# Three rotating PSUM tiles for the projections, three for the indexer logits, and the second half's gates moved ahead of branch B's pools

## The chip, the cores and the metric

The kernel runs on one core of a Trainium2 chip. The metric is the device time of one execution in microseconds, the median of several runs. The engines are named as in the profile: PE (TensorE), DVE (VectorE), ACT (ScalarE), POOL (GpSimd) and SP (SyncE, which issues the DMAs). Each engine takes its own instructions in the order in which the program lists them.

## What is computed

One layer over 2,048 tokens of width 1,024. A layer norm gives h; one projection of h (7,592 columns) feeds three branches and their gates; branch A attends to 256 keys per token that an indexer selects.

```
h = layer_norm(x)
a_q, a_k, a_v, a_gate, i_q, i_k, i_w, b_q, b_k, b_v, b_gate, c_q, c_gate, m_gate = split(h @ w_in)
# A: 8 heads over the top 256 keys of an indexer score
score = einsum('bqh,bqhs->bqs', i_w, relu(einsum('bqhd,bsd->bqhs', i_q, i_k)))   # chunk-causal
idx   = top_k(score, 256)
o_a   = softmax(a_q @ a_k[idx]) @ a_v[idx]
# B: differential attention, 4 heads;  C: attention into 256 memory tokens, 4 heads
merged = sum of sigmoid(m_gate[r]) * ((o_r * silu(gate_r)) @ w_proj[r])
out    = layer_norm(2**0.25 * h + merged @ w_out)
```

## The kernel before

**Stages.** The 16 blocks of 128 tokens are taken in two halves. For each half the kernel transposes h into H4 (`prologue`), projects the queries and the indexer (`dense_ai`), projects keys, values and queries of branch B (`dense_b`) and later the gates (`gates`). Every product of 32-bit accuracy is three matmuls (`mm3`, lines 77 to 79). A projection's result stands in a PSUM tile called dps; ACT and DVE read it out, and then the tile is free for the next projection. One tile of the gates takes 24 matmuls of 512 columns.

**The top-k search.** `topk_group` is called three times: for blocks 2 to 7, 8 to 11 and 12 to 15. A call has three parts. First the indexer logits: a PE matmul pair into a PSUM tile called ips (line 514), a Relu by ACT (line 519), and an accumulation into sall by DVE (line 523). Then a search of 32 passes for the threshold, one bit a pass: DVE counts for two of the blocks (line 550), ACT for the other two (line 563), and DVE forms the bit (line 567). At last a tie-break by block: POOL marks equal scores (line 595), DVE scans, selects and forms the mask (lines 598 to 601), and SP stores it (line 602). All this needs DVE, ACT and POOL; PE is needed for the logits alone. So the search stands beside projections, which keep PE busy meanwhile.

**What sets the order.** A scheduler orders each engine's instructions at build time from the program, its priorities and its own estimate of when a tile's buffer comes free; on the chip the order is fixed. Branch B's PE order is written out by hand (`tc.manual_schedule`). SP's queue holds all DMAs in one order.

**Around the change.** The projections' PSUM pool is `dqs` with 2 tiles (dps). `dq2` has 2 tiles for transposes (psT). `tq` has 4 tiles for the logits (ips), and `q1`, which stands there earlier, 4 for the first transposes. That is all 8 banks. After the third search comes `dense_b(1)`, then the pools are released, branch B's pools are made (`bp` in SBUF, `lgp` and `bs` in PSUM), then the second half's gates run, then four jobs of the first half's gates, and then branch B, whose first matmul is lg of line 655. Its keys kg, values vg and queries bq are loaded by SP into `bp`, which lies where the search's tiles lay.

Of the kernel before, what the change touches and what calls it, by code (L numbers as in the profile page):

```python
# [9 lines left out]
F32 = mybir.dt.float32  # L10
# [48 lines left out]
def tile_layer(ctx, tc, x, mem, ln_in_g, ln_in_b, w_in, w_mem_kv, diff_lambda, diff_norm_g,  # L59
# [101 lines left out]
    p1 = pool("p1", 3)  # L161
    dp = pool("dp", 2)
    dqs = pool("dqs", 2, PSUM)
    dq2 = pool("dq2", 2, PSUM)
    q1 = pool("q1", 2, PSUM, "right")
    xp = pool("xp", 8, side="right")
# [80 lines left out]
    def dense(kind, half, cols, idx, w=None):  # L247
        n = sum(c for _, c in cols)
        if w is None:
            w = load_win(cols, A if early[0] else G)  # L250
        for p in range(4 * half, 4 * half + 4):
            ps = dqs.tile([128, 2, 256], F32, name="dps")
            for i in range(2):
                h = hT_of(2 * p + i)
                for k in range(KT):
                    mm3(ps[:, i, :n], h[:, 0, k], h[:, 1, k], w[:, 0, k, :n], w[:, 1, k, :n], k == 0, k == KT - 1)
            with tc.high_priority():
                emit(kind, idx, p, ps, n)

    def gate_steps(kind, half, c0, idx, w=None, qs=(0, 1)):  # L260
        if w is None:
            w = load_win([(c0, 256)])
        for q in (2 * half + q for q in qs):
            for g in range(2):
                c = slice(g * 128, (g + 1) * 128)
                ps = dqs.tile([128, 512], F32, name="dps")
                for k in range(KT):
                    mm3(ps, w[:, 0, k, c], w[:, 1, k, c], H4[:, q % 2, 0, k], H4[:, q % 2, 1, k], k == 0, k == KT - 1)
                    if k == KT - 1:
                        with tc.high_priority():  # L270
                            emit_gate(kind, idx, g, q, ps)
                    yield 0.69

    def dense_ai01(half):
        W = []
        for i in range(2):
            if half == 0 and i:
                w = xw.tile([128, 2, 4, W_AI], F32R, name="w1", bufs=1)
            else:
                w = dw.tile([128, 2, KT, 256], F32R, name="w")  # L280
                w = w.rearrange("p a k c -> p (a k c)")[:, :8 * W_AI].rearrange("p (a k c) -> p a k c", a=2, k=4)
            W.append(w)
            if half:
                SP.dma_start(w.bitcast(F32), w_d["ai", i])
                continue
            for c0, cols in ((0, [(C_AK, 128), (C_IQ, 128)]), (256, [(C_IQ + 128, W_AI - 256)])):
                n = sum(c for _, c in cols)
                for k in (0, 2):
                    raw = dw.tile([128, 2, 256], F32, name="wr", bufs=2)
                    o0 = 0  # L290
                    for a0, an in cols:
                        SP.dma_start(raw[:, :, o0:o0 + an], w_view(w_in, i * 512 + k * 128, 2, a0, an))
                        o0 += an
                    split(w[:, 0, k:k + 2, c0:c0 + n], w[:, 1, k:k + 2, c0:c0 + n], raw[:, :, :n], A, G)
            w_d["ai", i] = dram(f"w_dai{i}", [128, 2, 4, W_AI])
            SP.dma_start(w_d["ai", i], w.bitcast(F32))
        for p in range(4 * half, 4 * half + 4):
            ps = [dqs.tile([128, 512], F32, name="dps") for _ in range(2)]
            for a in range(2):
                for i in range(2):  # L300
                    h = hT_of(2 * p + i)
                    for k in range(4):
                        kk = 4 * a + k
                        mm3(ps[i][:, :W_AI], h[:, 0, kk], h[:, 1, kk], W[a][:, 0, k], W[a][:, 1, k], kk == 0, kk == KT - 1)
            with tc.high_priority():
                o = [dw.tile([128, 2, 256], F32, name="do", bufs=3) for _ in range(2)]
                with tc.high_priority():
                    for i in range(2):
                        A.copy(o[0][:, i], ps[i][:, :256])
                        A.copy(o[1][:, i, :W_AI - 256], ps[i][:, 256:W_AI])  # L310
                emit("ai0", None, p, None, 256, o[0])
                emit("ai1", None, p, None, W_AI - 256, o[1])
# [97 lines left out]
    def run(steps):  # L410
        for _ in steps:
            pass
# [45 lines left out]
            W0 = load_win([(C_AQ, 256)], A, G, xw)  # L458
    SP.dma_start(rp, rope.rearrange("(b p) c -> p b c", p=128))
    for b in range(8):  # L460
        prologue(b, [(q1, "psT", 4)])
    dense_ai(0)
    rope0 = last_rope[0]
    xw.release()
    xp.release()
    q1.release()
    tk = pool("tk", 1, side="right")
    tq = pool("tq", 4, PSUM, "right")
    KI = {}

    def load_ki(half):
# [138 lines left out]
    for b in range(8, NB):  # L610
        load_x(b, p1)
        with tc.high_priority():
            prologue(b, [(tq, "ips", 4)])
    dense_ai(1)
    load_ki(1)
    topk_group([8, 9, 10, 11])
# [20 lines left out]

    dp.release()
    p1.release()
    dq2.release()  # L640

    bp = pool("bp", 2, side="right")
    lgp = pool("lgp", 2, PSUM, "right")
    turn = [0]
    bs = pool("bs", 1, PSUM, "right")
# [151 lines left out]
            G.tensor_scalar(o, o, rs, None, op0=ALU.mult)  # L797
            SP.dma_start(ob_d[b][:, hd * 128:(hd + 1) * 128], o)

    run(gates(1, JOBS[:-2]))  # L800
    run(gates_by_tokens(1, JOBS[-2:]))
    for p in range(4):
        with tc.high_priority():
            reload(p)
# [389 lines left out]
```

## Time and profile before

| | us |
|---|---|
| median of 3 runs | 2905.12 (2904.59 to 2905.88) |
| the profiled execution, its own time | 2899.8 |
| its span in the trace | 2898.0 |
| PE busy | 2767.6 (95%) |
| DVE busy | 2053.2 (71%) |
| ACT busy | 1401.0 (48%) |
| POOL busy | 861.0 (30%) |

The span is the time from the first to the last instruction that the trace shows; the execution's own time has 1.8 us around it. Matmuls overlap in their pipeline and the trace models their ends, so a busy PE can still hold short gaps. Times within the trace are counted from the span's start.

### The profile page before, as it was taken

Reading aid. Unit: us, or ns where it says so; the run is one execution under the profiler, and the core shown is the slowest. Engines: PE = TensorE matmul, PEld = TensorE weight load, DVE = VectorE, ACT = ScalarE, POOL = GpSimd, SP = SyncE. Lnnn points to the kernel's source line nnn. Section 1 sums busy time; section 2 is a strip of 40 time slices with the busy share of each in tenths; the row PEclk is TensorE's granted clock in tenths of the full one; section 3 lists DMA queues with packets and bytes.
Section 4 is the critical chain, followed back from the end, with each engine's and each line's share of the span. In section 5 each row is a group of like instructions: output and inputs, shape, how many; then the busy total and the mean of one; then the engine's idle time right before and its main releaser. Section 6 shows DMA issues by size and latency. Waiting matters only on the chain.

```text
span 2898.0 us, 49105 instructions
## 1 busy us (share of the span) xinstructions
PE 2767.6 (95%) x17488; PEld 2486.4 (86%) x17488; DVE 2053.2 (71%) x4885; ACT 1401.0 (48%) x2716; POOL 861.0 (30%) x1270
## 2 busy tenths in 40 slices
PE   7899999999999998999999999999999999988998
PEld 6799989987788877788878887888999999987887
DVE  7179977899657887577777773547777777775654
ACT  3256755774245881344444442446565655552110
POOL 7454333235433312023232323301222222211322
PEclk9999999999999999999999999999999999998999
DMA  9766654474645575534333425254333334358642
GB/s 359 237 211 233 206 185 165 157 251 149 219 151 174 203 275 182 175 107 130 128 118 113 146 80 171 91 178 133 103 112 104 104 114 124 115 175 262 210 153 73
DMA packets 332021, 476.35 MB, mean 164 GB/s; under 512 B 28929, under 2 KB 252545, under 8 KB 323585
## 3 DMA queue, kind: packets, MB, share of 16 engines
q1 hardware_dynamic: 331776, 473.23, 49.9%
q8 instruction: 138, 2.26, 0.3%
q14 instruction: 107, 0.87, 0.1%
HBM read 271.25 MB, written 201.88 MB: 163 GB/s over the span
## 4 chain that ended last, share of the span: by engine, by line
PE 68%; DMA 7%; DVE 7%; issue 3%; POOL 2%; ACT 2%; SPq 0%; DVEq 0%; POOLq 0%; ACTq 0%
PE dps L77 9%; PE dps L78 9%; PE dps L79 9%; PE ops L760 4%; PE aops L906 4%; PE apt L901 3%; PE lg L655 3%; PE lg L656 3%; PE pt L768 2%; PE yps L77 2%; PE yps L78 2%; PE yps L79 2%; PE fz L77 2%; PE fz L79 2%; PE fz L78 2%
## 5 line engine op out<-in xcount | busy, mean ns | idle before, releaser
L77 PE MATMUL dps<-H,w 128*128 128x512 f32 x1280 | 517.9, 405 | 20.8 <-DVE do L329 6.8
L78 PE MATMUL dps<-H,w 128*128 128x512 f32 x1280 | 504.9, 394 | 0.0
L79 PE MATMUL dps<-H,w 128*128 128x512 f32 x1280 | 503.7, 394 | 0.0
L77 PE MATMUL dps<-w,H 128*128 128x256 f32 (+1 forms) x1152 | 342.5, 298 | 16.3 <-ACT w L71 8.8
L79 PE MATMUL dps<-w,H 128*128 128x256 f32 (+1 forms) x1152 | 340.2, 296 | 2.0 <-DVE H L74 1.9
L78 PE MATMUL dps<-w,H 128*128 128x256 f32 (+1 forms) x1152 | 340.9, 296 | 0.8 <-POOL w L74 0.8
L563 ACT ACTIVATE ja<-sall,thr 128x1280 bf16<-128x1280 f32 (+4 forms) x224 | 301.8, 1347 | 74.5 <-DVE thr L559 69.0
L550 DVE TENSOR_SCALAR_CACHE_REDUCE jd<-sall,thr 128x1408 bf16<-128x1408 f32 (+6 forms) x231 | 330.8, 1432 | 6.3
L77 PEld LDWEIGHTS dps<-H,w 128*128 128x128 f32 x1280 | 243.3, 190 | 66.0 <-DVE do L329 7.4
L79 PEld LDWEIGHTS dps<-H,w 128*128 128x128 f32 x1280 | 242.7, 190 | 51.4
L78 PEld LDWEIGHTS dps<-H,w 128*128 128x128 f32 x1280 | 243.6, 190 | 38.2
L658 DVE CUSTOM_DVE_ANT_0 AP<-lg,bias 128x512 f32<-128x512 f32 (+3 forms) x304 | 181.7, 619 | 107.6 <-PE lg L656 50.2
L523 DVE SCALAR_TENSOR_TENSOR sall<-ir,iw,sall 128x512 f32<-128x512 f32 (+3 forms) x266 | 191.9, 768 | 70.0 <-ACT ir L519 67.5
L77 PEld LDWEIGHTS dps<-w,H 128*128 128x128 f32 x1152 | 224.0, 195 | 19.0 <-ACT w L71 9.4
L71 ACT CAST apr<-apt 128x512 fp32r<-128x512 f32 (+1 forms) x288 | 157.3, 562 | 153.2 <-PE apt L901 122.6
L79 PEld LDWEIGHTS dps<-w,H 128*128 128x128 f32 x1152 | 223.6, 194 | 3.3 <-DVE H L74 2.5
L78 PEld LDWEIGHTS dps<-w,H 128*128 128x128 f32 x1152 | 223.7, 194 | 2.6 <-POOL w L74 1.8
L74 DVE TENSOR_TENSOR apr<-apt,apr 128x512 fp32r<-128x512 f32 (+1 forms) x288 | 185.5, 656 | 56.7 <-ACT apr L71 54.9
L906 PE MATMUL aops<-apr,VA 128*128 128x256 f32 x1088 | 202.9, 294 | 11.8 <-DVE ao L916 6.2
L893 ACT ACTIVATE AP<-AP,anm 128x1024 f32<-128x1024 f32 (+7 forms) x192 | 172.2, 899 | 75.9 <-DVE anm L890 75.2
L519 ACT ACTIVATE ir<-ips 128x512 f32<-128x512 f32 (+3 forms) x304 | 149.9, 550 | 105.9 <-PE ips L514 91.5
L734 ACT ACTIVATE P<-P,nm 128x2048 f32<-128x2048 f32 (+15 forms) x128 | 154.4, 1206 | 85.8 <-DVE nm L733 85.7
(250 smaller groups left out, 6760.5 us busy)
## 6 DMA issues: line engine op xcount, KB each, us to landing
w_d<-w SPq DMA_DIRECT2D x28, 2048.0 KB, 7.3
w<-w_d SPq DMA_DIRECT2D x28, 2048.0 KB, 9.0
wr<-in_w_in_dram SPq DMA_DIRECT2D x108, 256.0 KB, 3.2
tm_d<-do SPq DMA_DIRECT2D x96, 256.0 KB, 2.6
bq<-qb_d SPq DMA_DIRECT2D x128, 128.0 KB, 3.3
aq<-qa_d SPq DMA_DIRECT2D x128, 128.0 KB, 3.0
yt<-tm_d SPq DMA_DIRECT2D x64, 256.0 KB, 3.4
sg_d<-do SPq DMA_DIRECT2D x48, 256.0 KB, 2.7
```

What stands on the lines that cost most here:

```text
L71: A.copy(H, src)
L74: el.tensor_tensor(L, src, H.bitcast(F32), op=ALU.subtract)
L77: PE.matmul(ps, lH, rH, start=start, stop=False)
L78: PE.matmul(ps, lH, rL, start=False, stop=False)
L79: PE.matmul(ps, lL, rH, start=False, stop=stop)
L523: V.scalar_tensor_tensor(s[:, c0:c0 + cn], r[:, :cn], iw[:, h:h + 1], s[:, c0:c0 + cn], op0=ALU.mult, op1=ALU.add)
L550: V.tensor_scalar(jd[:, :L], sc[b], t.bitcast(F32)[:, i:i + 1], None, op0=op, op1=ALU.add, accum_out=dst[:, i:i + 1])
L563: A.activation(ja[:, :L], sc[b], AF.Sign, bias=thr.bitcast(F32)[:, i:i + 1], scale=-1.0, accum_out=cnt[:, i:i + 1])
L658: V.tensor_tensor_reduce(P[:, c0:c0 + cn], ps[:, :cn], bias[:, c0:c0 + cn], scale=-0.125, scalar=-LOW, op0=ALU.add, op1=ALU.min, accum_out ...
L734: A.activation(p[:, :L], p[:, :L], AF.Exp, bias=nm[:, c:c + 1], scale=-1.0, accum_out=sm[:, c:c + 1])
L893: A.activation(p[:, c0:c1], p[:, c0:c1], AF.Exp, bias=nm[:, e:e + 1], scale=-1.0, accum_out=sm[:, hd, i:i + 1])
L906: PE.matmul(o_ps.rearrange("p a d -> p (a d)"), VA[:, k0 + i], pr[:, a, i].rearrange("p e q -> p (e q)"), start=(k0 + i == 0 and a == 0), ...
```

## The change

A helper `bank` gives the projections their PSUM tile: every third one is a new tile called dpx, one buffer in the pool `dq2`, and the others are dps as before. It does so until `spare[1]` is set to False, after the second half's gates. To make room, the logits have three ips tiles in place of four, and the early transposes three in place of four. The second half's gates are written ahead of the release of `dq2`, so ahead of branch B's PSUM pools; `bp` is now made ahead of them.

```diff
--- before.py
+++ after.py
@@ -161,6 +161,14 @@
     p1 = pool("p1", 3)
     dp = pool("dp", 2)
     dqs = pool("dqs", 2, PSUM)
+    spare = [0, True]
+
+    def bank(shape):
+        spare[0] += 1
+        if spare[1] and spare[0] % 3 == 0:
+            return dq2.tile(shape, F32, name="dpx", bufs=1)
+        return dqs.tile(shape, F32, name="dps")
+
     dq2 = pool("dq2", 2, PSUM)
     q1 = pool("q1", 2, PSUM, "right")
     xp = pool("xp", 8, side="right")
@@ -249,7 +257,7 @@
         if w is None:
             w = load_win(cols, A if early[0] else G)
         for p in range(4 * half, 4 * half + 4):
-            ps = dqs.tile([128, 2, 256], F32, name="dps")
+            ps = bank([128, 2, 256])
             for i in range(2):
                 h = hT_of(2 * p + i)
                 for k in range(KT):
@@ -263,7 +271,7 @@
         for q in (2 * half + q for q in qs):
             for g in range(2):
                 c = slice(g * 128, (g + 1) * 128)
-                ps = dqs.tile([128, 512], F32, name="dps")
+                ps = bank([128, 512])
                 for k in range(KT):
                     mm3(ps, w[:, 0, k, c], w[:, 1, k, c], H4[:, q % 2, 0, k], H4[:, q % 2, 1, k], k == 0, k == KT - 1)
                     if k == KT - 1:
@@ -295,7 +303,7 @@
             w_d["ai", i] = dram(f"w_dai{i}", [128, 2, 4, W_AI])
             SP.dma_start(w_d["ai", i], w.bitcast(F32))
         for p in range(4 * half, 4 * half + 4):
-            ps = [dqs.tile([128, 512], F32, name="dps") for _ in range(2)]
+            ps = [bank([128, 512]) for _ in range(2)]
             for a in range(2):
                 for i in range(2):
                     h = hT_of(2 * p + i)
@@ -458,14 +466,14 @@
             W0 = load_win([(C_AQ, 256)], A, G, xw)
     SP.dma_start(rp, rope.rearrange("(b p) c -> p b c", p=128))
     for b in range(8):
-        prologue(b, [(q1, "psT", 4)])
+        prologue(b, [(q1, "psT", 3)])
     dense_ai(0)
     rope0 = last_rope[0]
     xw.release()
     xp.release()
     q1.release()
     tk = pool("tk", 1, side="right")
-    tq = pool("tq", 4, PSUM, "right")
+    tq = pool("tq", 3, PSUM, "right")
     KI = {}
 
     def load_ki(half):
@@ -610,7 +618,7 @@
     for b in range(8, NB):
         load_x(b, p1)
         with tc.high_priority():
-            prologue(b, [(tq, "ips", 4)])
+            prologue(b, [(tq, "ips", 3)])
     dense_ai(1)
     load_ki(1)
     topk_group([8, 9, 10, 11])
@@ -637,9 +645,12 @@
 
     dp.release()
     p1.release()
+
+    bp = pool("bp", 2, side="right")
+    run(gates(1, JOBS[:-2]))
+    run(gates_by_tokens(1, JOBS[-2:]))
+    spare[1] = False
     dq2.release()
-
-    bp = pool("bp", 2, side="right")
     lgp = pool("lgp", 2, PSUM, "right")
     turn = [0]
     bs = pool("bs", 1, PSUM, "right")
@@ -797,8 +808,6 @@
             G.tensor_scalar(o, o, rs, None, op0=ALU.mult)
             SP.dma_start(ob_d[b][:, hd * 128:(hd + 1) * 128], o)
 
-    run(gates(1, JOBS[:-2]))
-    run(gates_by_tokens(1, JOBS[-2:]))
     for p in range(4):
         with tc.high_priority():
             reload(p)
```

How the order on the engines moves is shown at two places. The names carry the tiles' numbers, which are the same in both kernels; line numbers behind the new helper are 8 higher after the change, and 11 higher in branch B.

The first place is PE, the last indexer logits of the third group (ips_6803) among the second half's gates. Before:

```order
L514 MATMUL ips_6792<-KI3_1551,qi_6625 128x256
L77 MATMUL dps_10398<-H4_257,w_10379 128x512
L514 MATMUL ips_6797<-KI4_5198,qi_6625 128x256
L514 MATMUL ips_6797<-KI5_5200,qi_6625 128x256
L514 MATMUL ips_6803<-KI6_5202,qi_6625 128x256
L514 MATMUL ips_6803<-KI7_5204,qi_6625 128x256
L78 MATMUL dps_10398<-H4_257,w_10379 128x512
L79 MATMUL dps_10398<-H4_257,w_10379 128x512
```

And after the change:

```order
L79 MATMUL dpx_10943<-H4_257,w_10896 128x512
L77 MATMUL dpx_10943<-H4_257,w_10896 128x512
L522 MATMUL ips_6797<-KI4_5198,qi_6625 128x256
L522 MATMUL ips_6797<-KI5_5200,qi_6625 128x256
L522 MATMUL ips_6803<-KI6_5202,qi_6625 128x256
L522 MATMUL ips_6803<-KI7_5204,qi_6625 128x256
L78 MATMUL dpx_10943<-H4_257,w_10896 128x512
L79 MATMUL dpx_10943<-H4_257,w_10896 128x512
```

The last logits stand in the projection tile numbered 10398 before, and in tile 10943 now, 17 projection tiles further on. In the whole order 4,720 projection matmuls stand ahead of the last logit before, and 5,122 now; ahead of branch B's first lg stand 5,805 in both.

The second place is DVE, the tie-break of the third group. Lines 322 and 329 are evictions of projection tiles, line 550 a count. Before, for block 14:

```order
L550 TENSOR_SCALAR jd_6821,cnt_6818<-sall_6068,tf_7068 128x1920
L322 TENSOR_TENSOR do_11549<-dps_11521,do_11546 128x512
L597 TENSOR_SCALAR need_7073<-cnt_6818 128x1
L329 SCALAR_TENSOR_TENSOR do_11579<-do_11579,dps_11554 128x512
L598 SCALAR_TENSOR_TENSOR pf_6822<-ones_1541,ja_6820 128x1920
L329 SCALAR_TENSOR_TENSOR do_11608<-do_11608,dps_11583 128x512
L599 SCALAR_TENSOR_TENSOR ja_6820<-pf_6822,need_7073,ja_6820 128x1920
L600 TENSOR_TENSOR ja_6820<-ja_6820,jd_6821 128x1920
L601 TENSOR_SCALAR pf_6822<-ja_6820 128x1920
L550 TENSOR_SCALAR jd_6821,cnt_6818<-sall_6068,tf_7068 128x2048
L329 SCALAR_TENSOR_TENSOR do_11637<-do_11637,dps_11612 128x512
```

After the change, first the place where the last eviction ahead of branch B stands (line 337, tile dps_11816), among the search's passes:

```order
L558 TENSOR_SCALAR jd_6821,cnt_6818<-sall_6068,thr_6817 128x1920
L575 TENSOR_TENSOR bit_6819<-cnt_6818,lim_6811 128x4
L337 SCALAR_TENSOR_TENSOR do_11841<-do_11841,dps_11816 128x512
L576 SCALAR_TENSOR_TENSOR pre_6809<-bit_6819,pre_6809 128x4
L567 SCALAR_TENSOR_TENSOR thr_6817<-pre_6809,flip_6816 128x4
L558 TENSOR_SCALAR jd_6821,cnt_6818<-sall_6068,thr_6817 128x1664
L558 TENSOR_SCALAR jd_6821,cnt_6818<-sall_6068,thr_6817 128x1920
L575 TENSOR_TENSOR bit_6819<-cnt_6818,lim_6811 128x4
```

And after the change the end of the tie-break, for block 15, and the first instruction for branch B (lg_11876):

```order
L558 TENSOR_SCALAR jd_6821,cnt_6818<-sall_6068,tf_7068 128x2048
L605 TENSOR_SCALAR need_7073<-cnt_6818 128x1
L606 SCALAR_TENSOR_TENSOR pf_6822<-ones_1541,ja_6820 128x2048
L607 SCALAR_TENSOR_TENSOR ja_6820<-pf_6822,need_7073,ja_6820 128x2048
L608 TENSOR_TENSOR ja_6820<-ja_6820,jd_6821 128x2048
L609 TENSOR_SCALAR pf_6822<-ja_6820 128x2048
L674 TENSOR_SCALAR P_11875,mx_11872<-lg_11876 128x384
L676 ISA P_11875,mx_11872<-lg_11876,diag_249 128x128
L676 ISA mx_11872 128x1
L337 SCALAR_TENSOR_TENSOR do_11884<-do_11884,dps_11845 128x512
```

Before, 15 evictions stand from the search's last bit to branch B's first instruction, between the instructions of the tie-break and behind it. Now all of them stand ahead of the search's last four passes, and these passes and the whole tie-break follow behind the eviction of dps_11816 with nothing between. On SP the four mask stores stand likewise in a row, straight ahead of branch B's first key load, where before eleven stores of gates stood among them. PE has 21 matmuls of its next tile, dps_11845, between dps_11816 and the first lg, in both kernels.

## Rows read from the trace of the kernel before

**Rows 1.** Page, part 1: busy us, share of the span, instructions

```profile
PE 2767.6 (95%) x17488; PEld 2486.4 (86%) x17488; DVE 2053.2 (71%) x4885; ACT 1401.0 (48%) x2716; POOL 861.0 (30%) x1270
```

**Rows 2.** Waits of TensorE, 145 to 1181 us: total, times, longest

```profile
PE dps L77 <- DVE do L329: 6.8, 6, 2.0
...
PE dps L77 <- DVE do L322: 4.5, 2, 2.5
...
PE dps L77 <- DVE need L597: 4.3, 1, 4.3
...
PE dps L77 <- DVE de L74: 3.1, 2, 2.1
...
PE dps L77 <- DVE thr L559: 3.0, 1, 3.0
```

**Rows 3.** Line 514, logits of groups two and three: ns; first, last start

```profile
L514 PE MATMUL ips<-KI,qi x183: 219/280/388, 404.9 to 542.6; 128*128 128x256 f32 x166, 128*128 128x128 f32 x17
...
L514 PE MATMUL ips<-KI,qi x233: 221/279/283, 755.3 to 916.7; 128*128 128x256 f32 x105, 128*128 128x128 f32 x12
```

**Rows 4.** Line 602, bias stores of groups two and three

```profile
L602 SPq DMA_DIRECT2D bias_d<-pf x4: 319/380/586, 712.6 to 754.8; - x4
...
L602 SPq DMA_DIRECT2D bias_d<-pf x4: 319/320/933, 1110.9 to 1157.1; - x4
```

**Rows 5.** Chain of waits, 1080 to 1200 us: start, us, what

```profile
1098.57 4.49 POOL ja L595
...
1124.07 8.91 DMA bias_d<-pf
...
1141.91 5.45 POOL ja L595
...
1168.23 9.38 DMA kg<-kb_d
...
1177.62 4.92 DMA bq<-qb_d
...
1182.68 0.47 PE lg L656
```

**Rows 6.** Line 567, one bit of the third search each

```profile
L567 DVE TENSOR_TENSOR bit<-cnt,lim x32: 149/164/165, 924.6 to 1090.6; 128x4 int32<-128x4 f32 x32
```

**Rows 7.** Timeline of ScalarE near branch B: start, us, instruction

```profile
1170.71 0.60 ACT L327 ACTIVATE do<-dps 128x512 f32<-128x512 f32 x1 [4.84 <-PE dps L79]
...
1176.15 0.60 ACT L327 ACTIVATE do<-dps 128x512 f32<-128x512 f32 x1 [4.84 <-PE dps L79]
```

**Rows 8.** Timeline of VectorE, four counts and an eviction

```profile
1064.41 1.95 DVE L550 TENSOR_SCALAR_CACHE_REDUCE jd<-sall,thr 128x1664 bf16<-128x1664 f32 x1
...
1069.45 1.95 DVE L550 TENSOR_SCALAR_CACHE_REDUCE jd<-sall,thr 128x1664 bf16<-128x1664 f32 x1
...
1073.58 0.69 DVE L322 TENSOR_TENSOR do<-dps,do 128x512 fp32r<-128x512 f32 x1
...
1075.69 1.95 DVE L550 TENSOR_SCALAR_CACHE_REDUCE jd<-sall,thr 128x1664 bf16<-128x1664 f32 x1
```

**Rows 9.** Five lines of the last tie-break: ns of one, first, last start

```profile
L595 POOL TENSOR_SCALAR ja<-sall,tf x4: 4484/4956/5436, 1098.6 to 1141.9; 128x1664 bf16<-128x1664 f32 x1, 128x1792 bf16<-128x1792 f32 x1, 128x1920 bf16<-128x1920 f32 x1, 128x2048 bf16<-128x2048 f32 x1
...
L598 DVE TENSOR_TENSOR_SCAN pf<-ones,ja x4: 3625/4026/4425, 1103.1 to 1147.4; 128x1664 f16<-128x1664 bf16 x1, 128x1792 f16<-128x1792 bf16 x1, 128x1920 f16<-128x1920 bf16 x1, 128x2048 f16<-128x2048 bf16 x1
...
L599 DVE SCALAR_TENSOR_TENSOR ja<-pf,need,ja x4: 1952/2144/2347, 1106.7 to 1152.3; 128x1664 bf16<-128x1664 f16 x1, 128x1792 bf16<-128x1792 f16 x1, 128x1920 bf16<-128x1920 f16 x1, 128x2048 bf16<-128x2048 f16 x1
...
L600 DVE TENSOR_TENSOR ja<-ja,jd x4: 1015/1125/1225, 1109.2 to 1154.7; 128x1664 bf16<-128x1664 bf16 x1, 128x1792 bf16<-128x1792 bf16 x1, 128x1920 bf16<-128x1920 bf16 x1, 128x2048 bf16<-128x2048 bf16 x1
...
L601 DVE TENSOR_SCALAR pf<-ja x4: 594/643/689, 1110.3 to 1156.4; 128x1664 bf16<-128x1664 bf16 x1, 128x1792 bf16<-128x1792 bf16 x1, 128x1920 bf16<-128x1920 bf16 x1, 128x2048 bf16<-128x2048 bf16 x1
```

**Rows 10.** Windows, all engines: busy us, PEclk, DMA share, GB/s

```profile
1082.00:1086.00 4.00, 4.00 (x12) 3.12 (x11) 3.40 (x8) 2.71 (x5) 0.00 (x0) 0.57 0.94 388
...
1157.00:1182.00 25.00, 24.34 (x106) 19.59 (x104) 2.87 (x5) 2.40 (x4) 0.00 (x0) 0.99 0.95 263
```


## The prediction

> **What bounds the kernel now.** I read the page first. PE is busy 95% of the span [rows 1], so at first sight only PE's gaps could be won. The waits of TensorE between 145 us (where the first indexer logits come) and 1181 us (where branch B begins) show which gaps the rotation aims at: PE waited for DVE before a projection tile 6.8 + 4.5 + 4.3 + 3.1 + 3.0 = 21.7 us in all [rows 2]. That is everything a third tile could give back, apart from clock. After such a wait the granted clock can fall to half: around 1082 us, behind such a wait, the mean over 4 us is 0.57 [rows 10], between the two levels of 1.2 and 2.4 GHz, which costs 4 x 0.43 = 1.7 us. There are four such places in this part (near 727, 1082, 1109 and 1154 us), 7 us together.
>
> Then I read the search as a chain of its own, because it runs beside PE. It is a chain without slack. The last mask of group two is stored at 754.8 us [rows 4] and the first logit of group three starts at 755.3 [rows 3]. The last mask of group three is stored at 1157.1 [rows 4], SP then loads keys, values and queries, and the second lg matmul runs at 1182.7, having waited for bq [rows 5]. The chain of waits of that stretch goes through POOL, the mask store and the loads, not through PE alone [rows 5]. So at 1181 us two chains end together: PE's projections, and the search with its loads. A change is to be judged by both. The search can be late by next to nothing before PE waits for it, since PE's list goes on with lg and cannot pass it.
>
> **The change part by part.** *The third projection tile* can give back at most the 21.7 us of [rows 2]. Some of it counts only if it comes ahead of the search's last logits, because later the search decides. Of the five rows, 4.3 and 3.1 us and a part of the 6.8 and 4.5 lie earlier. I take 6 us, between 0 and 13.
>
> *The fourth logits tile* is what the change takes away, and the order shows what that does. The scheduler places a pair of logits where it thinks a tile is free; with three tiles it places them further apart. Counted in the order of PE, the last logit of group one comes behind 1,055 projection matmuls before and 1,225 now, that of group two behind 3,070 and 3,389, that of group three behind 4,720 and 5,122: each group falls further behind. These 402 matmuls are 16.75 tiles of 24. One tile takes 5.44 us on PE, the distance of two evictions by ACT [rows 7]. So the last logit, at 916.7 us before [rows 3], comes 16.75 x 5.44 = 91 us later, at 1008 us, and at 1002 with the 6 us above. That is the step on which the forecast rests. It is not a wait: PE works in between. But PE has only 5,805 - 5,122 = 683 projection matmuls left ahead of branch B, 683 / 24 x 5.44 = 155 us of cover, where it had 246.
>
> *What has to be done under that cover.* From the last logit to the search's first pass some 3 us pass (916.7 in [rows 3]; the first bit of the search at 924.6 [rows 6] is one pass behind it). A pass without an eviction on DVE takes 1069.45 - 1064.41 = 5.04 us, one with an eviction on it 1075.69 - 1069.45 = 6.24 us, in which 0.69 us are the eviction itself [rows 8]. Over the search the mean is (1090.6 - 924.6) / 31 = 5.36 us [rows 6]. In the new order 17 evictions stand on DVE among passes 11 to 28, where before three stood there at the end. I take 5.36 us for ten passes, 5.04 + 0.69 = 5.73 for eighteen and 5.04 for four: 54 + 103 + 20 = 177 us. Bounds: 32 x 5.04 = 161 and 32 x 6.24 = 200.
>
> *The tie-break.* From the last bit at 1090.6 [rows 6] to POOL's first mark at 1098.57 [rows 5] are 8.0 us, 7.3 without an eviction. A block then costs POOL 4.96, the scan 4.03, the selection 2.14, the add 1.13 and the mask 0.64 us [rows 9], one behind the other: 12.9 us, four times 51.6. Together 59 us. Before it took 1157.1 - 1090.6 = 66 us, with 15 evictions around it and one mask store that the next scan waited for 8.9 us [rows 5]; these are the bounds downward 56 and upward 66.
>
> *The loads.* From the last mask store to lg were 1182.7 - 1157.1 = 25.6 us [rows 4, 5], with stores of gates between them on SP's queue, the DMA engines busy 95% at 263 GB/s [rows 10]. Sixteen loads of keys and values of 0.26 MB and four of queries of 0.13 MB are 4.7 MB, 18 us at that rate. With no stores between I take 20, bounds 15 and 26.
>
> *The sum.* 1002 + 3 + 177 + 59 + 20 = 1261 us for the second lg, where it was 1182.7: 78 us later. From there the order on PE is the same through branch B, so the 78 us are not given back. Its four heads use dps and lg tiles as before; behind it, in branch A, the scheduler interleaves a little differently, which I take as nothing, give or take 3 us. A long idle time ends with the clock at half: 1.7 us for one stretch [rows 10]; I add 2. So 80 us on an execution of 2899.8, 2980. The median of the runs lies 5.3 us above that execution, which gives 2985.
>
> A check from PE's side: dps_11816 was evicted by ACT at 1176.15 [rows 7], and the four last passes and the tie-break now stand behind its eviction. If all of [rows 2] and the clock came back, 29 us, ACT is there at 1147, and lg runs at 1147 + 1.3 (both evictions) + 20 + 59 + 20 = 1247; if nothing came back, at 1276. The sum stands between them.
>
> *The gates' new place* costs nothing: the same 5,805 projection matmuls stand ahead of lg in both orders, and the loads into bp wait behind the mask stores on SP as before. *Three early transposing tiles for four* move the first logit by one projection matmul in the list, so nothing; its cover is the projection at hand, 5.44 us a tile.
>
> The Trainium skill (Perfetto Trace Analysis, Optimizing Tensor Performance, Matmuls) says that independent groups of matmuls should rotate through different PSUM banks, so that the evacuation of one overlaps the next group's matmuls. The waits of [rows 2] agree that two tiles are a little short. By that rule alone the change is a gain, the first rival below; it says nothing of the bank that the logits lose.
>
> **The rivals.** *Faster, by the rotation.* The waits go and the search is not late: 2905.1 - 21.7 - 7 = 2876. For it speaks that these waits are real. Against it speaks the fixed order: lg cannot run until four passes, a tie-break and the loads have followed the eviction of dps_11816. It decides only if these 20 + 59 + 20 = 99 us are covered, and the cover that the order leaves is the 21 matmuls of dps_11845, 5 us.
>
> *No change.* The search's late start would have to be caught up, 2905. Passes would have to take (177 - 78) / 32 = 3.1 us; the smaller of DVE's two counts in a pass alone takes 1.95 us [rows 8]. I see no mechanism.
>
> *Much slower.* Groups two and three also begin late, because each group's relu needs buffers that the tie-break before it holds (the same 0.5 us of slack [rows 3, 4]), all passes take 6.24 us, and the tie-break and loads take their upper bounds: 1008 + 5 + 3 + 200 + 66 + 26 = 1308, 125 us later, 3032. But group three's first pair moved by as many matmuls (3,075 to 3,392) as group two's last, so PE mostly reaches it when the tie-break is done; I give this end a small chance.
>
> **How the numbers follow.** The forecast with all its bounds between 2945 and 3020 has a chance of 0.88, the much slower end beyond that 0.05, the rivals no change and faster 0.03 each; 0.01 is left for an end between 2911 and 2945. Low bound of the sum: 995 + 3 + 161 + 56 + 15 = 1230, 47 us later, 2954 with 2 for the clock. A range of 8 in 10 goes from 2954 to 3016; its upper end takes the search at 190, tie-break 66 and loads 26 (1008 + 3 + 190 + 66 + 26 = 1293, 110 later). Faster or slower by 0.2% is about what a measurement of this kernel tells from no change. Faster 0.03, same 0.03, slower 0.94.
>
> **What would show it.** In the changed kernel's profile: the last logit at about 1002 us; the last bit of the third search near 1182; the last mask store near 1241; PE idle for some 80 to 100 us ahead of the first lg, released by a DMA of kg or bq, with a low clock there; PE's busy share near 93%; the five rows of [rows 2] shorter. The forecast is wrong if the last logit comes at about 920 us, if lg is released by PE's own work, or if the passes run far from 5.5 us.

## The result and the profile after

The changed kernel takes 2990.6 us (median of 4 runs, 2989.51 to 2995.33), the kernel before 2904.86 us on the same chip (4 runs, 2902.15 to 2905.88). The ratio is 1.0309, with a 95% interval from 1.0296 to 1.0323: it is slower by 86 us. The forecast was 2985, which is 80 us over the kernel before. The profiled execution after took 2990.04 us, with a span of 2988.3.

The page of the changed kernel, parts 1, 2 (the span in 40 slices, here the granted clock in tenths) and 4 (what the chain that ended last consists of):

```profile
span 2988.3 us, 49087 instructions
...
PE 2768.0 (93%) x17488; PEld 2489.5 (83%) x17488; DVE 2055.8 (69%) x4885; ACT 1404.3 (47%) x2716; POOL 873.2 (29%) x1270
...
PEclk9999999999999998599999999999999999998999
...
PE 71%; DVE 8%; DMA 8%; POOL 5%; issue 4%; ACT 2%; SPq 1%; POOLq 0%; DVEq 0%; ACTq 0%
```

PE is busy for as long as before, 2768.0 us against 2767.6 [rows 1], with the same number of instructions. The 90 us more of span are time in which PE stands still, nearly all of it in one place: the slice in which the clock digit is 5. The waits of TensorE from 145 us to branch B's first matmul name it (total, times, longest):

```profile
PE lg L666 <- DMA bq<-qb_d: 96.6, 1, 96.6
PE psT L227 <- POOL do L142: 11.4, 8, 2.7
PE ips L522 <- ACT ir L527: 8.6, 1, 8.6
PE dps L77 <- DVE thr L567: 3.0, 1, 3.0
PE dps L77 <- DVE do L337: 2.1, 1, 2.1
```

Read these against [rows 2]. Of the 21.7 us of waits for DVE before a projection tile, 5.1 are left: the third tile does what it is there for. But one wait of 96.6 us has come, on a load, and two smaller ones that are looked at below.

The search answers to [rows 3, 4, 6] as follows. The first two rows are the logits of groups two and three, then the bits and the mask stores of group three (in each, the two numbers behind the durations are the first and the last start). The last six matmuls of group two's row already fill group three's three tiles in advance, as seven did four tiles before:

```profile
L522 PE MATMUL ips<-KI,qi x182: 220/280/415, 408.2 to 583.0; 128*128 128x256 f32 x166, 128*128 128x128 f32 x16
...
L522 PE MATMUL ips<-KI,qi x234: 221/280/473, 793.4 to 1009.5; 128*128 128x256 f32 x113, 128*128 128x128 f32 x4
...
L575 DVE TENSOR_TENSOR bit<-cnt,lim x32: 152/163/395, 1016.6 to 1187.6; 128x4 int32<-128x4 f32 x32
...
L610 SPq DMA_DIRECT2D bias_d<-pf x4: 319/320/320, 1206.8 to 1247.4; - x4
```

Group three's logits begin 38 us later, at 793.4 for 755.3, and spread over 216 us where they took 161; everything behind them follows: the last logit comes 93 us later than before, the last bit 97, the last mask 90. In the chain of waits, which answers to [rows 5], there is no PE from here on (start, us, what):

```profile
1233.14 5.45 POOL ja L603
1238.61 4.44 DVE pf L606
1243.07 2.36 DVE ja L607
1245.46 1.24 DVE ja L608
1246.72 0.70 DVE pf L609
...
1249.81 5.46 DMA vg<-vb_d
1255.28 7.93 DMA vg<-vb_d
1263.23 5.81 DMA bq<-qb_d
1269.18 0.76 PE lg L667
```

The last block of the tie-break, one operation on POOL and four on DVE, then the loads, then lg. The windows show how empty the chip is meanwhile (stretch, length, then busy us of PE, PEld, DVE, ACT and POOL, granted clock, DMA share, GB/s):

```profile
1175.00:1247.00 72.00, 0.00 (x0) 0.00 (x0) 59.12 (x70) 10.42 (x12) 19.84 (x4) 0.50 0.05 19
1247.00:1268.00 21.00, 0.00 (x0) 0.00 (x0) 0.41 (x1) 0.00 (x0) 0.00 (x0) 0.50 0.99 254
1268.00:1276.00 8.00, 7.59 (x22) 5.77 (x23) 2.85 (x10) 0.60 (x1) 0.00 (x0) 0.64 0.34 87
1276.00:1290.00 14.00, 10.30 (x46) 8.38 (x45) 9.04 (x26) 5.60 (x7) 0.00 (x0) 0.91 0.06 21
```

### The profile page after: what moved, and what is told of

It is laid out like the page before. It is cut to its first block, busy times and chain, and to the rows that moved or that the text cites. A ratio compares the mean times of both kernels' runs of the same rounds, so it can differ in the third digit from the quotient of the medians.

```text
span 2988.3 us, 49087 instructions
## 1 busy us (share of the span) xinstructions
PE 2768.0 (93%) x17488; PEld 2489.5 (83%) x17488; DVE 2055.8 (69%) x4885; ACT 1404.3 (47%) x2716; POOL 873.2 (29%) x1270
## 4 chain that ended last, share of the span: by engine, by line
PE 71%; DVE 8%; DMA 8%; POOL 5%; issue 4%; ACT 2%; SPq 1%; POOLq 0%; DVEq 0%; ACTq 0%
PE dps L77 9%; PE dps L78 9%; PE dps L79 9%; PE ops L771 4%; PE aops L915 4%; PE apt L910 3%; PE lg L667 3%; PE lg L666 3%; PE dpx L78 2%; PE dpx L77 2%; PE dpx L79 2%; PE pt L779 2%; PE ips L522 2%; PE yps L77 2%; PE yps L78 2%
## 5 line engine op out<-in xcount | busy, mean ns | idle before, releaser
L77 PE MATMUL dps<-H,w 128*128 128x512 f32 x1064 | 432.4, 406 | 7.0 <-DVE thr L567 3.0
L78 PE MATMUL dps<-H,w 128*128 128x512 f32 x1064 | 419.7, 394 | 0.0
L79 PE MATMUL dps<-H,w 128*128 128x512 f32 x1064 | 418.2, 393 | 0.0
L531 DVE SCALAR_TENSOR_TENSOR sall<-ir,iw,sall 128x512 f32<-128x512 f32 (+3 forms) x266 | 198.1, 784 | 155.4 <-ACT ir L527 153.2
L79 PEld LDWEIGHTS dps<-H,w 128*128 128x128 f32 x1064 | 201.5, 189 | 42.7
L77 PEld LDWEIGHTS dps<-H,w 128*128 128x128 f32 x1064 | 202.2, 190 | 40.8 <-DVE thr L567 3.3
L79 PE MATMUL dps<-w,H 128*128 128x256 f32 (+1 forms) x776 | 229.6, 296 | 2.3 <-DVE H L74 2.3
L77 PE MATMUL dps<-w,H 128*128 128x256 f32 (+1 forms) x776 | 228.9, 296 | 1.2 <-ACT H L71 1.1
L78 PE MATMUL dps<-w,H 128*128 128x256 f32 (+1 forms) x776 | 229.4, 296 | 0.0
L78 PEld LDWEIGHTS dps<-H,w 128*128 128x128 f32 x1064 | 202.7, 191 | 29.7
L902 ACT ACTIVATE AP<-AP,anm 128x1024 f32<-128x1024 f32 (+7 forms) x192 | 172.2, 900 | 66.8 <-DVE anm L899 59.8
L74 POOL TENSOR_TENSOR w<-wr,w 128x512 fp32r<-128x512 f32 (+2 forms) x134 | 189.8, 1426 | 19.3 <-ACT w L71 15.1
L69 POOL TENSOR_SCALAR w<-wr 128x512 fp32r<-128x512 f32 x120 | 87.3, 735 | 368.1 <-PE dps L79 215.3
L666 PE MATMUL lg<-kg,bq 128*128 128x512 f32 (+3 forms) x214 | 79.5, 372 | 105.1 <-DMA bq<-qb_d 96.6
```

The source lines that it names most:

```text
L74: el.tensor_tensor(L, src, H.bitcast(F32), op=ALU.subtract)
L77: PE.matmul(ps, lH, rH, start=start, stop=False)
L78: PE.matmul(ps, lH, rL, start=False, stop=False)
L79: PE.matmul(ps, lL, rH, start=False, stop=stop)
L531: V.scalar_tensor_tensor(s[:, c0:c0 + cn], r[:, :cn], iw[:, h:h + 1], s[:, c0:c0 + cn], op0=ALU.mult, op1=ALU.add)
L666: PE.matmul(ps[:, :cn], q[0], k, start=True, stop=False)
```

## The experiments

My theory: the time is lost because the logits have one tile less. The scheduler then places the last logits 402 projection matmuls later, and the search, its tie-break and the loads stand open ahead of lg. Rivals: that the rotation itself, or the early tiles, cost the time; and that the gates' new place does. Experiments 1 to 4 ran on one chip, where the kernel before takes 2903.34 us (19 runs), 5 to 8 on another, where it takes 2899.24 us (24 runs). Each ratio is to the kernel before on its own chip.

### 1. Only the logits lose a tile

The kernel before, with one bank of PSUM left empty:

```diff
-    tq = pool("tq", 4, PSUM, "right")
+    tq = pool("tq", 3, PSUM, "right")
...
-            prologue(b, [(tq, "ips", 4)])
+            prologue(b, [(tq, "ips", 3)])
```

> The kernel before with three logits tiles in place of four and nothing else changed; one bank stays empty. Theory (fewer logits tiles spread the logits in PE's order, so the search ends late): the last logit stands behind 5,098 projection matmuls, 24 fewer than in the changed kernel, so branch B's first lg comes about 5 us earlier than there, near 1264 us, with one long PE wait of 85 to 97 us; time 2985 (2975 to 2995). Rival (the rotation of the projections or the place of the gates makes the loss): 2905, as before.

Measured: 3000.4 us (2995.54 to 3005.93), ratio 1.0335 (1.0315 to 1.0355). In its order the last logit stands behind 5,098 projection matmuls. Its rows of the logits and the mask stores:

```profile
L514 PE MATMUL ips<-KI,qi x234: 221/280/338, 789.4 to 1002.7; 128*128 128x256 f32 x113, 128*128 128x128 f32 x4
...
L602 SPq DMA_DIRECT2D bias_d<-pf x4: 320/320/320, 1200.2 to 1240.8; - x4
```

Its longest wait of TensorE ahead of branch B:

```profile
PE lg L655 <- DMA bq<-qb_d: 90.7, 1, 90.7
```

And the second lg in its chain of waits:

```profile
1261.62 0.76 PE lg L656
```

One part of the change, the logits' tile, gives nearly the whole loss at lg, with neither the rotation nor fewer early tiles nor the gates' new place: the second lg comes at 1261.6, 78.9 us later than before [rows 5] and 7.6 us ahead of the changed kernel's 1269.2. The wait and the place of lg are as expected. The time is not, it lies above the 2995 where the range ended: the span is 8.5 us longer than the changed kernel's (2996.8), because from branch A's first lg to the end it takes 1112.0 us, where the changed kernel takes 1095.9 and the kernel before 1093.9. These differences in branch A lie behind the place that is studied, and none of the runs tests where they come from.

### 2. The rotation with all four logits tiles

The changed kernel, but the bank for dpx is taken from the transposes (psT has one tile), and the logits keep four:

```diff
-        pt = dq2.tile([128, n, 2, 128], F32, name="psT")
+        pt = dq2.tile([128, n, 2, 128], F32, name="psT", bufs=1)
...
-        prologue(b, [(q1, "psT", 3)])
+        prologue(b, [(q1, "psT", 4)])
...
-    tq = pool("tq", 3, PSUM, "right")
+    tq = pool("tq", 4, PSUM, "right")
...
-            prologue(b, [(tq, "ips", 3)])
+            prologue(b, [(tq, "ips", 4)])
```

> The changed kernel with four logits tiles again; the bank is taken from the transposes of the projections' outputs, which get one tile in place of two. Theory: the last logit stands behind 4,686 projection matmuls, 34 fewer than before, the long wait is gone, and the rotation gives back a part of the 21.7 us of waits: 2885 to 2905. Rival (the rotation makes the loss): the long wait stays, 2985.

Measured: 2895.21 us (2890.33 to 2898.88, 10 runs), ratio 0.9972 (0.9962 to 0.9983). The last logit stands behind 4,686 matmuls. Its rows of the logits and the mask stores:

```profile
L522 PE MATMUL ips<-KI,qi x233: 221/279/582, 740.6 to 906.0; 128*128 128x256 f32 x105, 128*128 128x128 f32 x12
...
L610 SPq DMA_DIRECT2D bias_d<-pf x4: 319/320/320, 1101.6 to 1144.1; - x4
```

Branch B's first matmul in its timeline (in brackets the idle time before it, and what ended it):

```profile
1172.12 0.47 PE L666 MATMUL lg<-kg,bq 128*128 128x512 f32 x1 [0.46 <-DMA bq<-qb_d]
```

The rotation and the gates' place are both in this kernel, and it beats the kernel before by 8 us and the changed one by some 95. That either of them makes the loss is out: the loss is the logits' tile. PE comes to lg at 1172.1 and waits there for next to nothing, because the mask comes 13 us earlier as well; 12.7 of these stand already at group two's last mask (742.1 us, 754.8 before [rows 4]). How much of the small gain is PE's saved waiting is not shown: the last logit comes 10.7 us earlier, and the 34 matmuls by which it moved forward are 7.7 us of that at 5.44 us a tile. The same place in the timeline of the kernel before:

```profile
1181.24 0.47 PE L655 MATMUL lg<-kg,bq 128*128 128x512 f32 x1 [0.37 <-DMA bq<-qb_d]
```

### 3. Five tiles for the logits

If three tiles delay the search and four do not, does a fifth bring more? The kernel before, with the bank taken from the transposes:

```diff
-    dq2 = pool("dq2", 2, PSUM)
+    dq2 = pool("dq2", 1, PSUM)
...
-    tq = pool("tq", 4, PSUM, "right")
+    tq = pool("tq", 5, PSUM, "right")
...
-            prologue(b, [(tq, "ips", 4)])
+            prologue(b, [(tq, "ips", 5)])
```

> The kernel before with five logits tiles and one transposing tile; projections keep two tiles. Theory: the last logit stands behind 4,376 projection matmuls, 344 fewer than before, so the search ends some 75 us before PE comes to lg, lg is released by PE's own work, and the waits of projections for the tie-break's DVE work go: 2880 to 2895. Rival (the search had no part in the time of before, only PE's own waits): 2905 or a little more, for the one transposing tile.

Measured: 2937.82 us (2930.25 to 2939.77), ratio 1.0121 (1.0104 to 1.0139): a miss, and on the wrong side. The last logit stands behind 4,376 matmuls. Its rows of the logits and the mask stores:

```profile
L514 PE MATMUL ips<-KI,qi x231: 221/281/385, 737.9 to 857.1; 128*128 128x256 f32 x104, 128*128 128x128 f32 x12
...
L602 SPq DMA_DIRECT2D bias_d<-pf x4: 319/320/382, 1055.4 to 1106.4; - x4
```

Branch B's first matmul in its timeline:

```profile
1205.44 0.39 PE L655 MATMUL lg<-kg,bq 128*128 128x512 f32 x1
```

Four windows on the way there (columns as in the windows above):

```profile
145.00:400.00 255.00, 237.64 (x1927) 234.93 (x1927) 218.82 (x490) 170.88 (x368) 104.98 (x170) 0.98 0.60 201
400.00:600.00 200.00, 190.55 (x1507) 188.74 (x1506) 170.99 (x327) 127.43 (x234) 71.09 (x111) 0.98 0.51 171
...
1050.00:1100.00 50.00, 40.09 (x165) 31.01 (x164) 30.96 (x21) 4.08 (x7) 23.47 (x9) 0.93 0.81 278
1100.00:1150.00 50.00, 43.02 (x173) 34.08 (x172) 10.35 (x10) 3.65 (x7) 0.00 (x0) 0.93 1.00 326
```

The same windows of the kernel before:

```profile
145.00:400.00 255.00, 246.26 (x1985) 243.75 (x1984) 220.51 (x480) 169.75 (x369) 108.12 (x185) 1.00 0.62 205
400.00:600.00 200.00, 195.17 (x1537) 191.60 (x1537) 161.56 (x309) 115.46 (x215) 65.58 (x110) 0.98 0.54 179
...
1050.00:1100.00 50.00, 43.46 (x183) 34.86 (x182) 44.49 (x79) 33.09 (x38) 1.43 (x1) 0.97 0.85 297
1100.00:1150.00 50.00, 47.14 (x200) 38.21 (x199) 37.30 (x33) 4.74 (x8) 18.40 (x4) 0.97 0.52 186
```

The half of the theory that speaks of the search holds: with three, four and five tiles the last mask is stored at 1240.8, 1157.1 and 1106.4 us. What was wrong is that an earlier mask would buy time: PE must do the same work ahead of lg either way and comes to lg by itself, without a wait there, 24 us later than before. The windows show two places where it falls behind. Between 145 and 600 us PE is busy 8.6 + 4.6 = 13.2 us less. Between 1050 and 1150 us it is busy 3.4 + 4.1 = 7.5 us less, at a clock of 0.93 for 0.97, and from 1100 us on the DMA engines are busy all the time (1.00 at 326 GB/s for 0.52 at 186): branch B's loads now run beside the gates' weights and stores, and the longest wait of PE from 1000 us to lg is for weights:

```profile
PE dps L77 <- DMA w<-w_d: 7.3, 1, 7.3
```

In the kernel before that row has 1.0 us in the same stretch. Not all of the loss lies ahead of lg: from branch A's first lg to the end this kernel takes 1105.2 us, 11.3 more than before, and branch B gives 5 back. Experiment 7 takes up the first place.

### 4. The rotation for the gates alone

The kernel before, with the gates moved as in the change, and every third gate tile taken from psT's two tiles, which stand unused by then. PE's order ahead of lg is that of before:

```diff
+    def bank(shape):
+        spare[0] += 1
+        if spare[1] and spare[0] % 3 == 0:
+            return dq2.tile(shape, F32, name="psT")
+        return dqs.tile(shape, F32, name="dps")
...
-                ps = dqs.tile([128, 512], F32, name="dps")
+                ps = bank([128, 512])
...
+    spare[1] = True
+    run(gates(1, JOBS[:-2]))
+    run(gates_by_tokens(1, JOBS[-2:]))
+    spare[1] = False
+    dq2.release()
```

> The kernel before with the second half's gates ahead of branch B's pools and every third of their tiles taken from the transposes' two tiles, which stand idle there; logits keep four tiles, and the order on PE up to lg is that of before. Theory (two chains end together at lg, and the search's is as long as before): PE's waits before projection tiles fall by 5 to 15 us, but the wait ahead of lg grows by the same, since the mask stores come no more than 5 us earlier: 2897 to 2906. Rival (PE's waits alone set the time, the rotation is worth what it takes away): 2885 to 2895.

Measured: 2905.7 us (2901.13 to 2909.96, 10 runs), ratio 1.0008 (0.9997 to 1.0019): no effect. Its mask stores:

```profile
L610 SPq DMA_DIRECT2D bias_d<-pf x4: 319/319/320, 1114.8 to 1160.0; - x4
```

Branch B's second matmul in its timeline (the first runs at 1183.6 without a wait):

```profile
1184.80 0.47 PE L668 MATMUL lg<-kg,bq 128*128 128x512 f32 x1 [0.81 <-DMA bq<-qb_d]
```

The time is as expected, but the way to it is not. PE's waits for DVE before a projection tile fall by 5.9 us, from 21.7 to 15.8, and one of 4.9 us for ScalarE ahead of the logits comes in their place; the wait ahead of lg, which was to grow by 5 to 15 us, is 0.8. PE thus did not get ahead of the search here. The mask is stored at 1160.0 and at 1157.1 before [rows 4], a delay that is there already at group two's last mask (757.8 for 754.8), and the second lg runs 24.8 us behind it, 25.6 before. That a third tile for the gates pays by itself, 2885 to 2895, is out; what PE's saved waiting would be worth if the search stood still is not shown.

### 5. The tie-break taken off the chain

If the search is the chain now, then work taken from its end must come back almost in full. The changed kernel, without the tie-break of group three:

```diff
             e, g, m = ja[:, :L], jd[:, :L], pf.bitcast(BF16)[:, :L]
+            if blocks[0] == 12:
+                count(i, b, tf, ALU.is_gt, cnt)
+                V.tensor_scalar(m, g, -NEG, NEG, op0=ALU.mult, op1=ALU.add)
+                SP.dma_start(bias_d[b], m)
+                continue
```

> The changed kernel without the tie-break of the third group: equal scores are not marked, scanned or selected, so masks of blocks 12 to 15 keep only keys above the threshold. Left out a block: POOL's mark 4.96, the scan 4.03, the selection 2.14 and the add 1.13 us, 12.3 us, four times 49 us. Theory (PE waits ahead of branch B for the search's last DVE and POOL work, one for one): the long wait falls from 97 to about 48 us and the time from 2990 to 2942 (2935 to 2950). Rival (the wait is for the loads or for something else in branch B's start): within 5 us of the changed kernel.

Measured: 2944.9 us (2942.62 to 2950.74), ratio 1.0158 (1.0138 to 1.0178), as expected. The waits of TensorE, first row:

```profile
PE lg L671 <- DMA bq<-qb_d: 55.1, 1, 55.1
```

The wait shrinks by 41.5 us from 96.6, and the kernel's ratio by 0.0151, 44 us. Expected were 49 for the wait; the difference is the count that is left. In the tie-break it runs beside POOL's mark; here it stands alone, 2.1 us a block, 8.6 in all, and 49 - 8.6 = 40.4. Little else moved (the last logit runs at 1007.6 for 1009.5), so this is a direct sight of the chain: within some 3 us, a microsecond less on POOL and DVE is a microsecond less of the whole.

### 6. Only the gates' place

The kernel before, with the second half's gates ahead of branch B's PSUM pools:

```diff
+    run(gates(1, JOBS[:-2]))
+    run(gates_by_tokens(1, JOBS[-2:]))
+    dq2.release()
...
-    run(gates(1, JOBS[:-2]))
-    run(gates_by_tokens(1, JOBS[-2:]))
```

> The kernel before with the second half's gates written ahead of branch B's PSUM pools, and nothing else. Theory: the last logit stands where it did, behind 4,720 projection matmuls, and the search and PE come to lg as before: 2905 within 5 us. Rival (the place of the gates costs part of the loss): 2920 or more.

Measured: 2898.98 us (2894.65 to 2903.09, 10 runs), ratio 0.9999 (0.9987 to 1.0011). The kernel before is at 2899.24 on this chip, so this part of the change costs nothing and brings nothing. The last logit stands behind 4,720 matmuls and runs at 917.0, 916.7 before [rows 3].

### 7. One tile for the transposes

What of experiment 3's loss is the bank that the transposes gave? The kernel before, with that alone:

```diff
-    dq2 = pool("dq2", 2, PSUM)
+    dq2 = pool("dq2", 1, PSUM)
```

> The kernel before with one tile in place of two for the transposes of the projections' outputs, one bank left empty. It prices what the versions with four and five logits tiles pay for their bank. Theory (one transposing tile is nearly enough): the last logit stands behind 4,729 projection matmuls, 2 us later, 2903 to 2912, so that the 35 us lost with five logits tiles come from the logits themselves or the order around them. Rival (the single transposing tile makes those 35 us): 2925 to 2940.

Measured: 2914.62 us (2910.37 to 2915.93), ratio 1.0048 (1.0029 to 1.0066), 2.6 us beyond the end that I gave to the theory. The last logit stands behind 4,729 matmuls. Its mask stores:

```profile
L602 SPq DMA_DIRECT2D bias_d<-pf x4: 319/320/320, 1125.5 to 1168.3; - x4
```

Branch B's first matmul in its timeline:

```profile
1189.79 0.77 PE L655 MATMUL lg<-kg,bq 128*128 128x512 f32 x1 [7.36 <-DMA bq<-qb_d]
```

Of experiment 3's 35 us, 15 can thus be had with one transposing tile and four logits tiles. They come by another way, however: the mask is 11 us late, and PE waits 7.4 us at lg, which experiment 3 does not do. About 7 of the 15 lie behind lg, in branch A (1100.6 us, 1093.9 before). The first place of experiment 3 is not explained by this tile either: between 145 and 600 us PE is busy 2.8 us less than before, there 13.2. The other 20 us come only with five logits tiles, which pack the logits closely ahead of the projections and start the loads 50 us earlier. Whether these two are the cause, and how they share the 20 us, stays open.

### 8. The rotation over four tiles

If three tiles in experiment 2 give 0.28%, a fourth might give the rest. To experiment 2, the gates' other tile from psT:

```diff
+        if spare[2] and spare[0] % 3 == 1:
+            return dq2.tile(shape, F32, name="psT", bufs=1)
...
+    spare[2] = True
...
-    spare[1] = False
+    spare[1] = spare[2] = False
```

> The version with three rotating projection tiles, four logits tiles and one transposing tile, in which the second half's gates also use the idle transposing tile, so that they rotate over four. Theory (the search decides when lg can run; its last logit stands behind 4,710 projection matmuls, 24 more than with three tiles): no gain over the 2895 of that version, 2893 to 2902. Rival (PE's waits for projection tiles still cost): 2885 to 2890.

Measured: 2906.42 us (2898.97 to 2910.34, 12 runs), ratio 1.0017 (1.0005 to 1.0029): a miss, slower than experiment 2 by some 0.45%. Its mask stores:

```profile
L612 SPq DMA_DIRECT2D bias_d<-pf x4: 319/320/597, 1115.1 to 1160.2; - x4
```

Its wait at lg:

```profile
PE lg L669 <- DMA bq<-qb_d: 3.6, 1, 3.6
```

The mask comes at 1160.2, where experiment 2 has it at 1144.1, and now PE waits at lg. 13.9 us of that stand already at group two's last mask (756.0 for 742.1) and again at the last logit (919.9 for 906.0), where the order alone accounts for 24 matmuls, 5.4 us. The chain of waits ahead of that mask runs through POOL, which works on weights there and follows two loads of them, before its last mark:

```profile
723.11 9.03 DMA wr<-in_w_in_dram
...
738.07 3.64 DMA wr<-in_w_in_dram
```

So the search decides here too, from group two on. Why POOL met these loads in this version and not in experiment 2 was not tested.

## Why the prediction was right, point by point

**The logits (1002 us forecast, 1009.5 measured).** The step on which the forecast rested, 402 matmuls further back in the order, at 5.44 us for 24, holds: 916.7 + 91 = 1008. The trace divides it: group three's first logits behind the prefilled tiles stand behind 4,133 projection matmuls before and 4,311 now, so 178 of the 402 are spent by then and 224 between its logits, 40 and 51 us at that pitch; measured are 38 and 55. With the last logit behind 5,098 and 4,686 matmuls (experiments 1 and 2) the same sum gives 1002.4 and 909.0 us, measured 1002.7 and 906.0. With 4,376 (experiment 3) it gives 838.7, measured 857.1: there PE itself had fallen behind, and the pitch alone is 18 us off. The mis-sized term is the 6 us that the third tile was to save ahead of the last logit. It saved nothing. The waits for DVE before a projection tile went, as forecast, but others came: 8.6 us before group three's logits, and 11.4 us for POOL before the transposes' psT, where the kernel before has 4.9. The first of them was named in the prediction, under the rival much slower, as a thing of small chance. ScalarE's timeline in the changed kernel shows the relu that PE waited for:

```profile
792.80 1.58 ACT L527 ACTIVATE ir<-ips 128x512 f32<-128x512 f32 x3 [18.57 <-DVE ja L608]
```

And this is the row of the mask stores of group two in it:

```profile
L610 SPq DMA_DIRECT2D bias_d<-pf x4: 320/688/1207, 750.9 to 793.4; - x4
```

The relu of group three's logits waited until DVE had done the last add of group two's tie-break. It ran at 792.8 and read the first of the tiles filled in advance; the first logits behind these follow on PE at 793.4, when group two's last mask is stored. (What the prediction calls the first logit of group three is that place, too.) So the 0.5 us of slack between the groups [rows 3, 4] did not hold. In every kernel here group three's first logits run within 3 us of group two's last mask. Read so, the search is one chain through the groups, and a delay in group two is handed on.

**The search (177 us and 3 ahead of it forecast, 178.1 in all measured).** From the last logit at 1009.5 to the last bit at 1187.6 are 178.1 us, 1.9 less than forecast. The sum is right, the passes in it are rougher: by the timeline those without an eviction on DVE took 4.9 to 5.5 us (two 6.1 and 6.4), those with one 5.3 to 6.5, the two with two 6.4 and 8.5, and 7.1 us in place of 3 + 5 lie ahead of the first bit. One link between the chains the prediction did not see. In the kernel before, 16 passes in a row take 5.44 us, as long as a projection tile: in each of them ScalarE has an eviction among its counts, and waits for PE's tile before it:

```profile
962.37 0.60 ACT L327 ACTIVATE do<-dps 128x512 f32<-128x512 f32 x1 [0.94 <-PE dps L79]
```

In the changed kernel the last four passes, with PE idle, take 4.91 us.

**The tie-break (59 forecast, 59.8 measured).** 1247.4 - 1187.6. The chain of waits above shows the single pieces, with 5.45, 4.44, 2.36, 1.24 and 0.70 us for the last and largest block. Experiment 5 takes the first four out, and the time follows.

**The loads (20 forecast, 21.8 measured).** 1269.2 - 1247.4. They ran at 254 GB/s, a little under the 263 of [rows 10] that I used, with the DMA engines busy 99% and nothing else on them. The 4.7 MB of the forecast leave out four loads of queries: SP issues eight of them ahead of lg, 5.2 MB in all, which is 20.6 us at the measured rate. That the 20 came so near is in part luck.

**lg and what follows (80 us forecast, 90 in the span).** The second lg is 86.5 us later than before, forecast were 78: 7.5 too few for the logits, 1.9 too many for the search, 0.8 and 1.8 too few for the tie-break and the loads. Behind it the span grows by 3.8 us more, where I had 2 for the clock. The windows after show 8 us at 0.64 and 14 at 0.91. In the kernel before, the same two stretches behind the first lg have 1.00 and 0.88:

```profile
1181.00:1189.00 8.00, 6.79 (x29) 5.45 (x30) 3.63 (x12) 1.03 (x2) 0.00 (x0) 1.00 0.94 300
1189.00:1203.00 14.00, 10.31 (x44) 8.44 (x43) 9.06 (x25) 5.53 (x7) 0.00 (x0) 0.88 0.17 66
```

So the idle stretch costs clock in the first 8 us alone, at most 8 x 0.36 = 2.9 us. Of the 3.8 us, 1.8 lie in branch B and 2.0 in branch A. The median of all runs grew by 86 us, because the profiled execution before was one of the shorter ones and the one after was not: between profiled executions the forecast of 80 is 10 us short, between medians 6, and that difference is luck. That the time is not given back by the end was the last point at stake, and it is not.

**The rivals.** *Faster, by the rotation* has a part of the mechanism right and its price wrong: where the logits keep their tiles, the version with the rotation gains 8 us (experiment 2), not 29, and not all of it is shown to be the rotation's. In experiments 4 and 8 the mask does not come earlier, and neither does the time. PE's win ahead of lg can count only as far as the mask comes earlier too; but in experiment 4 PE won nothing there and in experiment 8 not more than 3.6 us, so this rests on the order more than on the runs. *No change* and *much slower* did not come; of the latter one part did, 8.6 us of it.

The Trainium skill (Perfetto Trace Analysis, Optimizing Tensor Performance, Matmuls) has independent matmul groups rotate through PSUM banks. Here the runs agree in part: with a bank taken from the transposes the rotation's version is 0.28% faster (experiment 2), with banks that stand idle there is no difference (experiment 4), and a fourth tile comes without the gain (experiment 8). They also show the other side: with the bank taken from the logits the kernel is 3.1% slower.

**What stays open.** Whether the close logits and the early loads make experiment 3's other 20 us, and in which parts; what of experiment 2's gain is the rotation and what the earlier logits; and why branch A takes up to 18 us longer in one kernel than in another (1093.9 before, 1112.0 in experiment 1), which only the traces compare. That the scheduler spreads the logits because it counts on a tile's release is inferred from the order with three, four and five tiles; its estimate itself was not looked at.

## What to carry to other kernels

Where two chains end together, ask of each PSUM tile which chain it feeds: the waits at the engine that looks busy show what a tile may give there (here at most 8 of the 29 us that were counted), not what it takes from the chain beside it (here 90 us). Where the order is fixed at build time, a buffer count moves instructions, and the change in the place of the last one times the pitch of the work ahead of it gives the delay before anything runs (91 us for 93 here), as long as that work itself runs as before (in experiment 3 it did not, and the sum was 18 us off). Getting a chain's result earlier than its consumer can use it brought nothing here: in experiment 3 the mask came 51 us earlier and the kernel was slower, by a cause that is only in part known.

## What the runs showed of the hardware

From 1175 to 1268 us, 93 us in which PE had nothing to do, the granted clock stood at 0.50, the lower of its two levels (1.2 GHz). Over the first 8 us of work behind it the mean is 0.64, and over the next 14 it is 0.91, where the kernel before, without an idle stretch, has 0.88: these 93 us cost at their end no more than some 3 us of clock. The loads that nothing disturbed did not run faster for it: 254 GB/s at a DMA share of 0.99, where experiment 3's ran at 326 GB/s together with the gates' transfers at a share of 1.00.
